# Gathering expert rows on one core: products moved from VectorE to GpSimd and ScalarE, rows fetched singly, and the paces of the side work redrawn

## The chip, the core and the metric

One NeuronCore of a Trainium2 chip runs the whole program. The metric is device time in microseconds from the first to the last instruction, a little more with what the launch adds. The engines are TensorE (PE, its weight loads as PEld), VectorE (DVE), ScalarE (ACT), GpSimd (POOL) and SyncE (SP, which issues most DMAs). Each engine takes its instructions strictly in the order that was written for it at build time; they wait for each other through semaphores.

## The reference, cut to what matters

Two blocks follow each other on 256 tokens of width 1024. The first has two layers of a three-part mixer and a feed-forward part (width 4096). The second has two layers of attention between the latent tokens `x` and 256 context tokens `xc`, each followed by a layer of 16,384 small experts, of which every token uses 128:

```python
def peer_block(hb, w_q, sub_keys, u_tab, v_tab):      # hb: tokens x 1024
    q = (hb @ w_q).reshape(n, 8, 256)
    s1, s2 = q[..., :128] . sub_keys[0], q[..., 128:] . sub_keys[1]
    ...                                               # top 16 of each, top 16 of the sums
    g = softmax(top_s)                                # 8 heads x 16 experts a token
    act = gelu(einsum('nhkd,nd->nhk', u_tab[expert], hb))
    return einsum('nhk,nhkd->nd', g * act, v_tab[expert])

for i in range(2):                                    # second block
    mod  = silu(c) @ ada_w[i] + ada_b[i]              # shifts, scales, gates for x
    modc = silu(c_ctx) @ ada_w[i] + ada_b[i]          # and for the context
    ...                                               # attention of x and, in layer 0, of xc
    x = x + g2 * peer_ffn(h2, ...)
    if i == 0:
        xc = xc + cg2 * peer_ffn(h2c, ...)
```

## The kernel before, in words

**Foreground.** `tile_two_blocks` writes the program in this order: mixer 0, feed-forward 0 ("ffn 0"), mixer 1, ffn 1, then `block2`: the attention of layer 0, its expert layer, and the same for layer 1. The experts are not looked up: all 128x128 of them are computed densely, one column of 128 at a time. `ahead` (line 1130) runs through 128 such columns e = 0 to 127: `hidden` loads 512 KB of the table u, splits it in two parts (ScalarE casts it, line 209, VectorE subtracts, line 210), multiplies it on TensorE with 384 tokens (24 matmuls of 384 columns, lines 243 to 245), applies GELU on ScalarE (line 1126) and stores the result. Beside it `choose` picks the experts, and `spread` (32 groups of 4 tokens for each 128 tokens) writes the gate table G: four comparisons a group on GpSimd (line 1071), four VectorE instructions (line 1075), eight small matmuls (line 1089) and a copy (line 1090). `experts` then weighs the stored columns with G and multiplies them with the table v.

**Side work.** Of the 256 context tokens, 128 join the 256 latent ones in these 384. The other 128 take the way of the reference: `gather` (line 1275), with one token on each partition. For each of the 128 choices a token has, one indirect DMA on GpSimd's queue (line 1286) fetches a row of u for every token, 128x1024 f32; VectorE multiplies it with the token's vector `h` and sums along the row into one number (line 1304). After GELU and gate, 128 rows of v are fetched in the same way, and VectorE adds each, times its number, to an accumulator (line 1308). Two rows share one place of 128x2x1024 and are fetched together, a pair ahead. `context`, `context_end`, `context_scores`, two `choose`, one `spread` and `gather` form one generator, `aside`; the foreground takes steps of it wherever it says `breathe`, or at the rates that the tables WM, WF, FN and GP give. `ada_rest` forms the modulation numbers: one 512 KB load and a VectorE product with sum (line 777) for each of 128 columns and vector.

**What sets the order.** A scheduler takes the instructions in the order in which the Python code wrote them as a priority, and fixes a sequence for each engine; an instruction whose inputs seem ready may be put ahead of older ones of the foreground. At run time nothing is reordered. The pool tags say how many places a tile has: `b8` 3 places of 8 KB a partition, `k8` 7, `wb` 3, `ws` 4 (two pairs of split weights).

Of the functions that the change touches:

Of the kernel before, what the change touches and what calls it, by code (L numbers as in the profile page):

```python
# [39 lines left out]
P0 = ((0, 1.0), (22, 1.0), (30, 0.8), (72, 0.8))  # L40
P1 = ((2, 1.0), (28, 0.8), (30, 0.72), (79, 0.8))

GP = (0.85, 0.6)
# [14 lines left out]
class Net:  # L58
    def __init__(self, ctx, tc, io):
        self.tc, self.nc, self.io = tc, tc.nc, io  # L60
        self.cst = ctx.enter_context(tc.tile_pool(name="cst", bufs=1))
        self.sb = ctx.enter_context(tc.tile_pool(name="sb", bufs=1))
        self.ps = ctx.enter_context(tc.tile_pool(name="ps", bufs=1, space=bass.MemoryType.PSUM))
        self.dr = ctx.enter_context(tc.tile_pool(name="dr", bufs=1, space=bass.MemoryType.DRAM))
        self.x = self.cst.tile([P, 2, D], F32, tag="x", name="x")
        for b in range(2):
            tc.nc.sync.dma_start(self.x[:, b], io["x"][b * P:(b + 1) * P])
        self.bufs = {"w": 4, "ws": 4, "wb": 3, "b8": 3, "b12": 2, "k8": 7, "k4": 4, "k2": 6, "b2": 3}
        self.pbufs = {"A": 2, "B": 2, "C": 4}
        self.uid = 0  # L70
        self.ring, self.turn = ("ws",), 0
        self.fg = Side("w", True, "C", "A", "k8", "k4", "k2", "f")
# [659 lines left out]
    def new_mod(self, l):  # L732
        self.mod = self.t("mod", [P, 2, 48], bufs=2)
        self.adab = self.load("adab", [P, 48], self.io["ada_b"][l], bufs=2)
        self.gn = self.load("gn", [P, 2, KC], self.io["norm2"][l], bufs=2)

    def ada_early(self):
# [17 lines left out]
        nc.vector.tensor_copy(self.mod[:, :, 0:EARLY], pt.rearrange("p f s -> p s f"))  # L755

    def ada_rest(self, i0, i1):

        nc, io = self.nc, self.io
        if i0 < 48 - 8:  # L760
            both = self.t("b12", [P, 2, D])
            cb = [both[:, i] for i in range(2)]
        else:
            cb = [self.t("kv", [P, D], bufs=2) for _ in range(2)]
# [3 lines left out]
        for i in range(i0, i1):  # L768
            l, f = divmod(i, 48)
            if f == 0:  # L770
                self.new_mod(1)
            w = self.load("wb", [P, D], io["ada_w"][i - EARLY])
            for s in range(2):
                if l and s and f >= 16:
                    continue
                junk = self.t("b2", [P, D], mybir.dt.bfloat16)
                nc.vector.scalar_tensor_tensor(junk, w, 1.0, cb[s], ALU.mult, ALU.mult, accum_out=self.mod[:, s, f:f + 1])
            if i == 47:
                nc.vector.tensor_add(self.mod[:, :, MID:], self.mod[:, :, MID:], self.adab[:, None, MID:].to_broadcast([P, 2, 48 - MID]))
            yield  # L780

    def modulation(self, l, part):

        nc, mod = self.nc, self.mod
        lo, hi, j, g = ((0, 16, 8, 0), (16, 48 if l else MID, 32, 1))[part]
        ns = 1 if l == 1 and part == 1 else 2
        for s in range(ns):
            nc.vector.tensor_add(mod[:, s, lo:hi], mod[:, s, lo:hi], self.adab[:, lo:hi])
            nc.vector.scalar_tensor_tensor(mod[:, s, j:j + 8], mod[:, s, j:j + 8], 1.0, self.gn[:, g], ALU.add, ALU.mult)
# [412 lines left out]
    def context(self):  # L1202
# [3 lines left out]
        mod = self.mod0 = self.mod  # L1206
# [5 lines left out]
        rest = self.ada_rest(EARLY, MID)  # L1212
# [62 lines left out]
    def gather(self, idx, g, out):  # L1275


        nc, io = self.nc, self.io
        tables = io["u_rows"], io["v"][0].rearrange("a b d -> (a b) d")
        work = [(t, c) for t in tables for c in range(0, P, 2)]  # L1280

        def fetch(i):
            t, c = work[i]
            r = self.t("b8", [P, 2, D])
            for j in range(2):
                nc.gpsimd.indirect_dma_start(out=r[:, j], out_offset=None, in_=t,
                                             in_offset=bass.IndirectOffsetOnAxis(ap=idx[:, c + j:c + j + 1], axis=0))
            return r

        hr = self.t("b8", [P, 2, D])  # L1290
        nc.sync.dma_start(hr[:, 0], self.hrd)
        h, acc = hr[:, 0], hr[:, 1]
        act = self.t("act", [P, P], bufs=1)
        r = fetch(0)
        for i, (t, c) in enumerate(work):
            if i == P // 2:
                nc.scalar.activation(act, act, AF.Gelu_apprx_tanh)
                nc.vector.tensor_mul(act, act, g)
            nxt = fetch(i + 1) if i + 1 < len(work) else None
            for j in range(2):  # L1300
                a = act[:, c + j:c + j + 1]
                if i < P // 2:
                    junk = self.t("b2", [P, D], mybir.dt.bfloat16)
                    nc.vector.scalar_tensor_tensor(junk, r[:, j], 1.0, h, ALU.mult, ALU.mult, accum_out=a)
                elif i == P // 2 and j == 0:
                    nc.vector.tensor_scalar(acc, r[:, j], a, None, ALU.mult)
                else:
                    nc.vector.scalar_tensor_tensor(acc, r[:, j], a, acc, ALU.mult, ALU.add)  # L1308
                yield
            r = nxt  # L1310
        nc.sync.dma_start(out, acc)
        yield

    def aside(self):


# [8 lines left out]
        yield from self.gather(idx, g, self.accd)  # L1325

    def block2(self, x):
# [7 lines left out]
        self.beside(self.attn_out(fg, 0, oT, col(mod, 0, 2), x), FN[3])  # L1335
        hx = self.norm_T(fg, x, col(mod, 0, 4), col(mod, 0, 3), lambda k: (h[0][:, k, 0:S], h[1][:, k, 0:S]))
        hd = lambda k: (h[0][:, k], h[1][:, k])
        far = self.side
        plan = self.routing(0, [hx], Gd[0], ((0, 0), (1, 8)), EAR[0], P0)
        self.ahead(0, hd, ND, self.kept, 128, plan + [(0, far, GP[0], False), (100, self.ada_rest(MID, 48), 0.3, True)])  # L1340
# [3 lines left out]
        rest, due = self.ada_rest(48, 96), [0.0]  # L1344

        def side(e):
            if e % 2:
                next(rest, None)
# [12 lines left out]
        mod = self.mod  # L1361
# [119 lines left out]
def tile_two_blocks(ctx: ExitStack, tc: tile.TileContext, io: dict, out: bass.AP):  # L1481
    net = Net(ctx, tc, io)
    x, net.out = net.x, out
    net.kept = net.dr.tile([128, P, ND], F32, tag="kept0", name="kept0")
# [24 lines left out]
```

## Time and profile before

| | us |
|---|---|
| median of 3 runs | 3633.68 |
| lowest, highest | 3614.31, 3634.95 |
| the profiled execution | 3624.63 |
| its span, first to last instruction | 3622.9 |

| engine | busy us | share of the span |
|---|---|---|
| PE | 3248.7 | 90% |
| PEld (beside PE) | 2772.2 | 77% |
| DVE | 2513.4 | 69% |
| ACT | 1449.4 | 40% |
| POOL | 978.2 | 27% |

Shares of the whole span hide the stages. In the trace, mixer 0 and ffn 0 take the first 556 us, mixer 1 lasts to 764, ffn 1 to 1032, attention and key scores of layer 0 to 1332, the 128 columns of `ahead` to about 2066, the expert sums to 2642, and layer 1 the rest. The fetches of `gather` lie between 1023 and 1882 us.

### The profile page before, as it was taken

To read this page: it belongs to the slowest core of one execution; us is meant where nothing else is said; L and a number is where in the kernel's file an instruction comes from. 1 tells how busy PE (TensorE), PEld (TensorE's weight loads), DVE (VectorE), ACT (ScalarE), POOL (GpSimd) and SP (SyncE) were. 2 spreads that over 40 slices of the span, in tenths; PEclk is the share of its full clock that TensorE was granted. 3 is DMA by queue.
4 is the path that set the end of the run, shared out by engine and by line. 5 is a ranking of instruction groups with operands and counts; after the bars stand their busy time and mean duration, and the time that the engine had idled before them with its cause. 6 is when DMAs were issued, how large, how long until landed. Compare 5 with 4: busy or idle time off the path is not lost. (4 is left out here: it accounts for less than half of the span.)

```text
span 3622.9 us, 51227 instructions
## 1 busy us (share of the span) xinstructions
PE 3248.7 (90%) x18333; PEld 2772.2 (77%) x18333; DVE 2513.4 (69%) x5177; ACT 1449.4 (40%) x2465; POOL 978.2 (27%) x968
## 2 busy tenths in 40 slices
PE   8999899889756698887779899999989999999999
PEld 6676688768644597887779887777868999988777
DVE  6667556789667897887665576655577888656665
ACT  6543245633323342232223433333344555454443
POOL 0000000000954434787776000000010067830000
PEclk9999999979978899998889999999999999999999
DMA  7456454325467778887886788877523677688885
GB/s 241 151 180 204 151 164 146 108 89 172 159 223 245 253 267 300 291 290 266 287 274 228 254 283 276 266 251 251 178 66 101 198 243 264 241 281 291 288 258 188
DMA packets 340225, 803.17 MB, mean 222 GB/s; under 512 B 31105, under 2 KB 179585, under 8 KB 334593
## 3 DMA queue, kind: packets, MB, share of 16 engines
q1 hardware_dynamic: 303104, 665.66, 56.0%
q0 software_dynamic: 36864, 134.23, 10.8%
q8 instruction: 144, 2.36, 0.3%
q14 instruction: 113, 0.92, 0.1%
HBM read 713.00 MB, written 86.77 MB: 221 GB/s over the span
## 5 line engine op out<-in xcount | busy, mean ns | idle before, releaser
L209 ACT CAST ws<-w 128x1024 fp32r<-128x1024 f32 (+1 forms) x528 | 547.3, 1037 | 1048.8 <-PE psA L244 727.6
L210 DVE TENSOR_TENSOR ws<-w,ws 128x1024 fp32r<-128x1024 f32 (+1 forms) x528 | 640.7, 1215 | 255.3 <-ACT ws L209 253.5
L245 PE MATMUL psA<-b,ws 128*128 128x384 f32 (+1 forms) x2048 | 659.0, 322 | 105.2 <-DVE ws L210 104.3
L1071 POOL TENSOR_SCALAR wb<-iota,R 128x128 f16<-128x128 f16 x640 | 600.3, 954 | 382.3 <-ACT R L1054 279.1
L243 PE MATMUL psA<-b,ws 128*128 128x384 f32 (+1 forms) x2048 | 663.4, 324 | 3.6 <-ACT ws L209 3.6
L244 PE MATMUL psA<-b,ws 128*128 128x384 f32 (+1 forms) x2048 | 652.1, 318 | 0.0
L245 PEld LDWEIGHTS psA<-b,ws 128*128 128x128 f32 x2048 | 398.9, 195 | 119.9 <-DVE ws L210 118.7
L209 ACT CAST k<-wb 128x1024 fp32r<-128x1024 f32 x256 | 269.0, 1051 | 513.3 <-DMA wb<-in_v 513.2
L245 PE MATMUL psC<-k,k 128*128 128x512 f32 x1056 | 422.7, 400 | 25.9 <-DVE k L210 25.2
L243 PE MATMUL psC<-k,k 128*128 128x512 f32 x1056 | 418.6, 397 | 19.6 <-ACT k L209 19.6
L244 PE MATMUL psC<-k,k 128*128 128x512 f32 x1056 | 417.6, 396 | 3.6 <-DVE k L210 3.6
L243 PEld LDWEIGHTS psA<-b,ws 128*128 128x128 f32 x2048 | 399.8, 195 | 4.7 <-ACT ws L209 4.5
L244 PEld LDWEIGHTS psA<-b,ws 128*128 128x128 f32 x2048 | 398.4, 195 | 0.0
L210 DVE TENSOR_TENSOR k<-wb,k 128x1024 fp32r<-128x1024 f32 x256 | 312.4, 1220 | 81.9 <-ACT k L209 81.7
L158 POOL TENSOR_TENSOR rsrf<-rsvf,neghalf 128x1 f32<-128x1 f32 (+5 forms) x38 | 41.9, 1106 | 1206.6 <-DVE rsvf L157 1206.6
L244 PE MATMUL psC<-ws,k 128*128 128x512 f32 (+1 forms) x608 | 250.3, 412 | 25.5 <-DVE ws L210 25.4
L245 PEld LDWEIGHTS psC<-k,k 128*128 128x128 f32 x1056 | 199.2, 189 | 93.2 <-DVE k L210 49.4
L1165 DVE TENSOR_TENSOR k<-k,b 128x384 f32<-128x384 f32 (+1 forms) x256 | 123.7, 489 | 202.7 <-DMA k<-kept 197.8
L243 PE MATMUL psC<-ws,k 128*128 128x512 f32 (+1 forms) x608 | 246.9, 410 | 7.1 <-DVE k L197 4.5
L243 PEld LDWEIGHTS psC<-k,k 128*128 128x128 f32 x1056 | 199.5, 189 | 66.7 <-ACT k L209 23.8
L1308 DVE SCALAR_TENSOR_TENSOR b<-b,act,b 128x1024 f32<-128x1024 f32 x127 | 164.2, 1293 | 120.3 <-DMA b<-in_v,idx 119.7
L245 PE MATMUL psC<-ws,k 128*128 128x512 f32 (+1 forms) x608 | 246.1, 407 | 0.7 <-DVE k L716 0.6
(452 smaller groups left out, 6096.2 us busy)
## 6 DMA issues: line engine op xcount, KB each, us to landing
w<-in_u SPq DMA_DIRECT2D x256, 512.0 KB
wb<-in_v SPq DMA_DIRECT2D x256, 512.0 KB
w<-in_w_ff SPq DMA_DIRECT2D x128, 512.0 KB
wb<-in_ada_w SPq DMA_DIRECT2D x80, 512.0 KB
G<-k SPq DMA_DIRECT2D x32, 1024.0 KB
w<-in_wA SPq DMA_DIRECT2D x48, 512.0 KB
kept<-k SPq DMA_DIRECT2D x128, 192.0 KB
b<-G SPq DMA_DIRECT2D x16, 1536.0 KB
```

What stands on the lines that cost most here:

```text
L158: nc.gpsimd.tensor_tensor(r[:m, :cols], v[:m, :cols], self.neghalf[:m, :cols], op=ALU.pow)
L209: self.nc.scalar.copy(hi, src)
L210: self.nc.vector.tensor_sub(lo, src, hi.bitcast(F32))
L243: self.nc.tensor.matmul(out, ah, bh, start=first, stop=False)
L244: self.nc.tensor.matmul(out, ah, bl, start=False, stop=False)
L245: self.nc.tensor.matmul(out, al, bh, start=False, stop=last)
L1071: nc.gpsimd.tensor_scalar(first[:, j], self.iota16, r0[:, n + j:n + j + 1], None, ALU.is_equal)
L1165: nc.vector.tensor_mul(g3, g3, Gs[:, :, j])
L1308: nc.vector.scalar_tensor_tensor(acc, r[:, j], a, acc, ALU.mult, ALU.add)
```

## The change

- `gather` works on single rows. Four places of 128x1024 take turns, and the fetch for row i+2 is issued at row i.
- For a row of u, GpSimd multiplies it with `h` in place (`TENSOR_TENSOR`), and one step later ScalarE sums it (a copy with an accumulator). VectorE has no part in it.
- Of the rows of v, the even ones are added by VectorE as before; the odd ones are scaled by ScalarE and added by GpSimd into a second accumulator, and GpSimd adds the two at the end.
- The expert choice for the gathered tokens comes first, and the first 96 steps of `gather` run beside the second `choose` and the 32 loads of `ada_rest` for layer 1; they are all written ahead of the second norm of layer 0. The `spread` for the 128 context tokens moves from `aside` (ffn 1) into `ahead`, which now has three of them.
- WM, WF, FN, P0 and GP get other numbers; of the `ada_rest` of layer 1, 16 columns stay beside the expert sums (of 48).

```diff
-WM = ({3: 1, 5: 2, 12: 3, 22: 1, 34: 1}, {12: 2, 14: 2, 18: 2, 22: 2, 26: 2, 32: 2, 34: 2, 37: 2})
-WF = ((0, 2.0), (0, 3.5))
-FN = (4, 2.0, 2.0, 2.0)
+WM = ({3: 4, 4: 1, 5: 2, 9: 1, 11: 1, 12: 3, 14: 1, 16: 1, 18: 1, 20: 1, 22: 2, 24: 1, 26: 1, 30: 1, 32: 1, 34: 1},
...
+WF = ((0, 1.6), (0, 1.6))
+FN = (2, 1.8, 1.8, 1.8)
...
-    def gather(self, idx, g, out):
+    def gather(self, idx, g, hr):
...
+            def fetch(i):
+                if i < i1:
+                    nc.gpsimd.indirect_dma_start(out=places[i % 4], out_offset=None, in_=(u, v)[i // P],
+                                                 in_offset=bass.IndirectOffsetOnAxis(ap=idx[:, i % P:i % P + 1], axis=0))
+
+            def first(i):
+                r, c = places[i % 4], i % P
+                if i < P:
+                    nc.gpsimd.tensor_tensor(r, r, h, op=ALU.mult)
+                elif c % 2 == 0:
+                    nc.vector.scalar_tensor_tensor(acc[:, 0], r, act[:, c:c + 1], acc[:, 0], ALU.mult, ALU.add)
+                else:
+                    nc.scalar.activation(r, r, AF.Copy, scale=act[:, c:c + 1])
+
+            def second(i):
+                r, c = places[i % 4], i % P
+                if i < P:
                     junk = self.t("b2", [P, D], mybir.dt.bfloat16)
-                    nc.vector.scalar_tensor_tensor(junk, r[:, j], 1.0, h, ALU.mult, ALU.mult, accum_out=a)
...
+                    nc.scalar.activation(junk, r, AF.Copy, accum_out=act[:, c:c + 1])
+                elif c % 2:
+                    nc.gpsimd.tensor_tensor(acc[:, 1], acc[:, 1], r, op=ALU.add)
...
+            fetch(i0), fetch(i0 + 1)
+            for i in range(i0, i1):
+                if i > i0:
+                    second(i - 1)
+                fetch(i + 2)
...
+                first(i)
                 yield
...
         idx, g = yield from self.choose(self.rc, ss[1], True)
-        R = yield from self.choose(self.rc, ss[0])
-        yield from self.spread(R, self.Gd[0], 16, "B", "b8")
...
+        def weights():
+            self.R0 = yield from self.choose(rc8, ss[0])
+            yield from self.ada_rest(1, 16, 48, [hr[:, 1]])
...
+        for i, _ in enumerate(steps(0, NA, [two[i // 2][:, i % 2] for i in range(4)])):
+            next(also, None)
+            yield
...
-        self.ahead(0, hd, ND, self.kept, 128, plan + [(0, far, GP[0], False), (100, self.ada_rest(MID, 48), 0.3, True)])
+        plan += [(P0[4][0], self.spread(self.R0, Gd[0], 16), P0[4][1], True), (0, far, GP[0], False)]
+        self.ahead(0, hd, ND, self.kept, KEPT0, plan + [(96, self.ada_rest(0, MID, 48), 0.4, True)])
```

GpSimd's queue in ffn 1, before (`wb` holds a group's one-hot tiles, `iota` and `R` what they are compared from):

```order
L158 TENSOR_TENSOR rsrf_6646<-rsvf_6645,neghalf 128x1
L158 TENSOR_TENSOR rsrf_6652<-rsvf_6651,neghalf 128x1
L1071 TENSOR_SCALAR wb_8118<-iota_225,R_1535_8111 128x128 x4
L1071 TENSOR_SCALAR wb_8126<-iota_225,R_1535_8111 128x128 x4
L1071 TENSOR_SCALAR wb_8219<-iota_225,R_1535_8111 128x128 x4
L1071 TENSOR_SCALAR wb_8237<-iota_225,R_1535_8111 128x128 x4
```

The same stretch of GpSimd's queue now (`b_1381` and `k_1382` are the four row places, `b_1379` is `h`):

```order
L1293 DMA k_1382_7113<-in_u_rows,idx_7104 128x1024
L1299 TENSOR_TENSOR b_1381_7112<-b_1381_7112,b_1379_7109 128x1024
L1293 DMA k_1382_7113<-in_u_rows,idx_7104 128x1024
L1299 TENSOR_TENSOR b_1381_7112<-b_1381_7112,b_1379_7109 128x1024
L1293 DMA b_1381_7112<-in_u_rows,idx_7104 128x1024
L1299 TENSOR_TENSOR k_1382_7113<-k_1382_7113,b_1379_7109 128x1024
```

The 128 comparisons have gone from ffn 1 and the fetches and products of u, one of each in turn, stand in their place; before, the fetches of u began only behind the comparisons.

ScalarE's queue in ffn 1 now (line 216 is the cast that was line 209, line 1309 the row sum, line 721 a square of the foreground, line 714 before):

```order
L1309 ACTIVATE b_1569_8235,act_7111<-b_1381_7112 128x1024
L216 CAST ws_7497<-w_7495 128x1024
L1043 ACTIVATE k_1383_7118<-k_1383_7118 128x128
L1309 ACTIVATE b_1580_8317,act_7111<-b_1381_7112 128x1024
L216 CAST ws_7515<-w_7513 128x1024
L721 ACTIVATE k_1417_7319<-k_1439_7465 128x256
L721 ACTIVATE k_1417_7319<-k_1440_7470 128x256
L1309 ACTIVATE b_1581_8325,act_7111<-k_1382_7113 128x1024
L216 CAST ws_7543<-w_7541 128x1024
```

A row sum stands ahead of nearly every weight cast; before, casts and squares alone followed each other there. In the order now all 128 row sums stand ahead of the first column of `ahead`.

GpSimd's queue in the first half of `ahead` now (line 1311 is the add of an odd row of v, line 1076 the comparisons that were line 1071, `b_2032` and `b_2033` the row places):

```order
L1293 DMA b_2032_10222<-in_v,idx_7104 128x1024 x2
L1076 TENSOR_SCALAR wb_12147<-iota_225,R_1676_8902 128x128 x4
L1311 TENSOR_TENSOR b_1379_7109<-b_1379_7109,b_2033_10223 128x1024
L1293 DMA b_2033_10223<-in_v,idx_7104 128x1024 x2
L1076 TENSOR_SCALAR wb_12204<-iota_225,R_1676_8902 128x128 x4
L1311 TENSOR_TENSOR b_1379_7109<-b_1379_7109,b_2032_10222 128x1024
L1293 DMA b_2032_10222<-in_v,idx_7104 128x1024 x2
```

Before, this part of the queue held fetches of u and then of v, later with comparisons between them, and no product or sum; the comparisons of the third `spread` are new here.

## Rows read from the trace of the kernel before

**Rows 1.** Stretches: from:to, length, each engine's busy us, TensorE's granted clock, DMA share, GB/s
```profile
764.00:1032.00 268.00, 224.57 (x1427) 188.03 (x1425) 216.22 (x588) 102.37 (x148) 112.45 (x132) 0.94 0.50 163
1032.00:1332.00 300.00, 211.19 (x1032) 171.78 (x1033) 249.69 (x563) 99.99 (x216) 130.39 (x110) 0.82 0.74 251
1332.00:1641.00 309.00, 268.29 (x1501) 258.59 (x1500) 255.07 (x578) 96.82 (x143) 197.60 (x173) 0.93 0.84 287
1641.00:2071.00 430.00, 357.01 (x2088) 342.16 (x2086) 252.65 (x323) 136.77 (x204) 258.91 (x238) 0.92 0.78 263
2642.00:2816.00 174.00, 160.95 (x889) 135.75 (x889) 126.78 (x364) 87.76 (x219) 9.48 (x12) 0.96 0.29 93
```
**Rows 2.** TensorE's waits, 1332 to 1641, 1641 to 2071: us in total, times, longest
```profile
PE psA L245 <- DVE ws L210: 38.7, 16, 5.4
...
PE psA L245 <- DVE ws L210: 65.0, 22, 7.2
```
**Rows 3.** VectorE's groups in those two stretches: busy us, mean ns, idle us before
```profile
L1308 DVE SCALAR_TENSOR_TENSOR b<-b,act,b 128x1024 f32<-128x1024 f32 x56 | 72.3, 1291 | 33.9 <-DMA b<-in_v,idx 33.7
L1304 DVE SCALAR_TENSOR_TENSOR b<-b,b 128x1024 bf16<-128x1024 f32 x30 | 36.3, 1216 | 15.0 <-DMA b<-in_u_rows,idx 14.9
...
L1308 DVE SCALAR_TENSOR_TENSOR b<-b,act,b 128x1024 f32<-128x1024 f32 x71 | 92.0, 1295 | 86.4 <-DMA b<-in_v,idx 86.0
```
**Rows 4.** ScalarE's GELU, one a column: 1332 to 1640.6, 1640.6 to 2071
```profile
L1126 ACT ACTIVATE k<-psA 128x384 f32<-128x384 f32 x56 | 27.1, 485 | 0.0
...
L1126 ACT ACTIVATE k<-psA 128x384 f32<-128x384 f32 x72 | 35.0, 486 | 0.0
```
**Rows 5.** ScalarE, 1917.9 to 1992.5, then 2036.5 to 2061.9: columns, and groups of spread
```profile
L1126 ACT ACTIVATE k<-psA 128x384 f32<-128x384 f32 x16 | 7.8, 487 | 0.0
L1090 ACT ACTIVATE k<-psC 128x512 f32<-128x512 f32 x13 | 7.7, 592 | 0.0
...
L1126 ACT ACTIVATE k<-psA 128x384 f32<-128x384 f32 x6 | 2.9, 486 | 0.0
```
**Rows 6.** GpSimd's groups of the whole span, then the comparisons of ffn 1 alone
```profile
L1286 POOL DMA_INDIRECT b<-in_v,idx x128 | 165.3, 1291 | 106.4 <-DVE b L1308 51.4 <-issue 26.0 <-DVE k L946 16.0
L1286 POOL DMA_INDIRECT b<-in_u_rows,idx x128 | 157.4, 1230 | 222.3 <-DVE b L1304 137.6 <-DVE amxf L892 22.5 <-issue 20.1
...
L1071 POOL TENSOR_SCALAR wb<-iota,R 128x128 f16<-128x128 f16 x128 | 108.9, 869 | 133.8 <-ACT R L1054 133.5 <-POOL wb L1071 0.2
```
**Rows 7.** Lines 1071 and 210 alone: ns shortest/median/longest, first and last start
```profile
L1071 POOL TENSOR_SCALAR wb<-iota,R x640: 592/702/4086, 913.4 to 3209.8; 128x128 f16<-128x128 f16 x160
...
L210 DVE TENSOR_TENSOR ws<-w,ws x128: 1200/1219/1436, 1331.2 to 2062.2; 128x1024 fp32r<-128x1024 f32 x128
```
**Rows 8.** VectorE's 128-column cast (1500 to 1900 us) and its 128x1024 subtract (ffn 1)
```profile
L1016 DVE CAST k<-k 128x128 f32<-128x128 uint32 x4 | 1.0, 248 | 0.0
...
L210 DVE TENSOR_TENSOR ws<-w,ws 128x1024 fp32r<-128x1024 f32 x64 | 78.2, 1222 | 18.6 <-ACT ws L209 18.2
```
**Rows 9.** Line 713, the first VectorE instruction on each product of ffn 1
```profile
L713 DVE TENSOR_SCALAR k<-psA x32: 395/418/425, 796.1 to 1033.8; 128x256 f32<-128x256 f32 x32
```
**Rows 10.** VectorE in 1032 to 1332: the gathered rows' products, and the reads of their sums
```profile
L1304 DVE SCALAR_TENSOR_TENSOR b<-b,b 128x1024 bf16<-128x1024 f32 x97 | 117.8, 1222 | 38.5 <-DMA b<-in_u_rows,idx 38.5
L1304 DVE DVE_READ_ACCUMULATOR b<-b,b 128x1 f32 x97 | 8.2, 84 | 0.0
```
**Rows 11.** ScalarE: a 128x1024 cast in ffn 1, an accumulator's read in 1032 to 1332
```profile
L209 ACT CAST ws<-w 128x1024 fp32r<-128x1024 f32 x65 | 68.1, 1048 | 112.2 <-PE psC L244 50.1 <-PE psA L244 42.5 <-DVE ws L210 5.6
...
L839 ACT ACTIVATION_READ_ACCUMULATOR k<-psC 128x1 f32 x20 | 4.4, 221 | 0.0
```
**Rows 12.** TensorE's waits in the expert sums, 2071 to 2642
```profile
PE psC L245 <- DVE k L210: 18.2, 23, 2.0
PE psC L243 <- ACT k L209: 9.1, 3, 6.9
```
**Rows 13.** The page: GB/s in 40 slices of the span; the software queue (256 fetches): packets, MB
```profile
GB/s 241 151 180 204 151 164 146 108 89 172 159 223 245 253 267 300 291 290 266 287 274 228 254 283 276 266 251 251 178 66 101 198 243 264 241 281 291 288 258 188
...
q0 software_dynamic: 36864, 134.23, 10.8%
```

More of the change, by code (lines that the diff above doesn't have):

```diff
@@ L754, in ada_early, with ada_rest @@
             nc.tensor.transpose(pt[:, f], row[:, f * P:(f + 1) * P], self.ident[0:2, 0:2])
-        nc.vector.tensor_copy(self.mod[:, :, 0:EARLY], pt.rearrange("p f s -> p s f"))
-    def ada_rest(self, i0, i1):
+        nc.vector.tensor_copy(self.mods[0][0][:, :, 0:EARLY], pt.rearrange("p f s -> p s f"))
+    def ada_rest(self, l, f0, f1, cb=None):
         nc, io = self.nc, self.io
[L760 to L764, printed above, removed]
+        if cb is None:
+            if l == 0 and f0 < MID:
+                both = self.t("b12", [P, 2, D])
+                cb = [both[:, i] for i in range(2)]
+            else:
+                cb = [self.t("kv", [P, D], bufs=2) for _ in range(2)]
         for t, n in zip(cb, ("c", "c_ctx")):
@@ L767, in ada_rest @@
             nc.scalar.activation(t, t, AF.Silu)
[L768 to L775, printed above, removed]
+        if l not in self.mods:
+            self.new_mod(l)
+        mod, adab, _ = self.mods[l]
+        for f in range(f0, f1):
+            w = self.load("wb", [P, D], io["ada_w"][48 * l + f - EARLY])
+            for s, c in enumerate(cb):
                 junk = self.t("b2", [P, D], mybir.dt.bfloat16)
-                nc.vector.scalar_tensor_tensor(junk, w, 1.0, cb[s], ALU.mult, ALU.mult, accum_out=self.mod[:, s, f:f + 1])
-            if i == 47:
-                nc.vector.tensor_add(self.mod[:, :, MID:], self.mod[:, :, MID:], self.adab[:, None, MID:].to_broadcast([P, 2, 48 - MID]))
+                nc.vector.scalar_tensor_tensor(junk, w, 1.0, c, ALU.mult, ALU.mult, accum_out=mod[:, s, f:f + 1])
+            if l == 0 and f == 47:
+                nc.vector.tensor_add(mod[:, :, MID:], mod[:, :, MID:], adab[:, None, MID:].to_broadcast([P, 2, 48 - MID]))
             yield
     def modulation(self, l, part):
-        nc, mod = self.nc, self.mod
+        nc, (mod, adab, gn) = self.nc, self.mods[l]
         lo, hi, j, g = ((0, 16, 8, 0), (16, 48 if l else MID, 32, 1))[part]
@@ L1211, in context @@
         yield
-        rest = self.ada_rest(EARLY, MID)
+        rest = self.ada_rest(0, EARLY, MID)
         def both():
@@ L1309, in gather @@
                 yield
-            r = nxt
-        nc.sync.dma_start(out, acc)
-        yield
+            second(i1 - 1)
+        return steps
     def aside(self):
+        nc = self.nc
         yield from self.context()
@@ L1321, in aside @@
         idx, g = yield from self.choose(self.rc, ss[1], True)
-        R = yield from self.choose(self.rc, ss[0])
-        yield from self.spread(R, self.Gd[0], 16, "B", "b8")
+        hr = self.t("b8", [P, 2, D])
+        nc.sync.dma_start(hr[:, 0], self.hrd)
+        steps = self.gather(idx, g, hr)
+        rc8 = Side("wb", True, "B", "B", "k8", "wb", "b2", "b", "wb", "b2")
+        def weights():
+            self.R0 = yield from self.choose(rc8, ss[0])
+            yield from self.ada_rest(1, 16, 48, [hr[:, 1]])
+        also = weights()
+        two = [self.t(t, [P, 2, D]) for t in ("b8", "k8")]
+        for i, _ in enumerate(steps(0, NA, [two[i // 2][:, i % 2] for i in range(4)])):
+            next(also, None)
+            yield
+        self.done(also)
+        self.early = True
+        yield
+        two = [self.t("b8", [P, 2, D]) for _ in range(2)]
+        yield from steps(NA, 2 * P, [two[i // 2][:, i % 2] for i in range(4)])
         self.accd = self.dr.tile([P, D], F32, tag="accd", name="accd")
-        yield from self.gather(idx, g, self.accd)
+        nc.gpsimd.tensor_tensor(hr[:, 0], hr[:, 0], hr[:, 1], op=ALU.add)
+        nc.sync.dma_start(self.accd, hr[:, 0])
+        yield
     def block2(self, x):
@@ L1335, in block2 @@
         self.beside(self.attn_out(fg, 0, oT, col(mod, 0, 2), x), FN[3])
+        far = self.side
+        while not self.early:
+            next(far)
         hx = self.norm_T(fg, x, col(mod, 0, 4), col(mod, 0, 3), lambda k: (h[0][:, k, 0:S], h[1][:, k, 0:S]))
         hd = lambda k: (h[0][:, k], h[1][:, k])
-        far = self.side
         plan = self.routing(0, [hx], Gd[0], ((0, 0), (1, 8)), EAR[0], P0)
-        self.ahead(0, hd, ND, self.kept, 128, plan + [(0, far, GP[0], False), (100, self.ada_rest(MID, 48), 0.3, True)])
+        plan += [(P0[4][0], self.spread(self.R0, Gd[0], 16), P0[4][1], True), (0, far, GP[0], False)]
+        self.ahead(0, hd, ND, self.kept, KEPT0, plan + [(96, self.ada_rest(0, MID, 48), 0.4, True)])
         gates = self.t("k8", [P, 4, 512])
```

62 lines of the change are left out of this document (25 added, 37 removed).

## The prediction, made before the changed kernel ran

> **What bounds the kernel now.** I read the table of stretches first [rows 1]. Its five engine columns are TensorE, its weight loads, VectorE, ScalarE and GpSimd; then come the granted clock, the share of the DMA engines' time and GB/s. VectorE leads in the attention of layer 0 (1032 to 1332 us), TensorE elsewhere, but TensorE is not full in the first half of `ahead`, from 1332 to 1641 us (268 of 309), and in the second half (357 of 430). GpSimd is not full anywhere: 112 of 268 us in ffn 1, 198 of 309 and 259 of 430 in `ahead`. So I asked what TensorE waits for in `ahead` [rows 2]: the weight split that VectorE does, 38.7 and 65.0 us. Why VectorE is late stands in its own groups [rows 3]: in the queue ahead of the splits are the multiply-adds of gathered rows, and before those VectorE sat idle for fetches: 33.9 + 15.0 us in the first half, 86.4 in the second. A late row thus holds the split, and the split holds TensorE. That is what the change can win.
>
> What can it win at most? The GELU, one a column, counts columns [rows 4]: 56 up to 1640.6, 72 after it. After the gather is over, 6 columns without a group of `spread` took 25.4 us, or 4.23 each, and 16 columns with 13 groups 74.6 us [rows 5], so a group adds (74.6 − 16×4.23)/13 = 0.53. All 128 columns with the 64 groups of now would take 575 us at that pace, and they took 730.
>
> **The change part by part.** What GpSimd must do before which column I read off the built order, by following what each instruction needs back through the queues. Between the first square of ffn 1 (796.1 us, from [rows 9], where line 713 starts at once on the first finished product) and the first GELU of `ahead` (1332.2), GpSimd now has 120 fetches of u, 8 of v, 124 products and 16 comparisons. From there to the GELU of column 56 it has 116 fetches of v, 58 adds and 212 comparisons. Behind that are 156 comparisons in 39 groups and no gather.
>
> Prices: a fetch of u 1.23, of v 1.29, and a comparison 0.869 as in ffn 1 [rows 6]. A GpSimd product or sum of 128x1024 f32 stands nowhere in the trace, so I bound it. Low end: VectorE's own 1.22 for such a product [rows 10]. High end: eight comparisons of 128 columns at 0.592, the shortest of them, as if none of it were a fixed cost: 4.74 [rows 7]. A middle by ratio, the root of 1.22×4.74, is 2.40; another one, GpSimd's 592 ns against VectorE's 248 ns on 128 columns [rows 8], times 1.22, is 2.92. I take 2.40 for the product by itself, and add the wait that the comparisons of ffn 1 had beside VectorE, 0.869 − 0.592 = 0.28: **2.68**.
>
> Term 1, from 796.1 to 1332.2: 120×1.23 + 8×1.29 + 16×0.869 = 172 of GpSimd, and 124×2.68 = 332 more: 504 for the 536 of before, **−32**. That it is GpSimd which ends this stretch follows from what is left of the others. VectorE had 224.6 + 249.7 in the two stretches, of which 126.0 go (97 products and the reads of their sums, [rows 10]); the part behind 796.1 is some 224.6×236/268 + 123.7 = 322. The DMAs of ffn 1 become 64 weights, some 75 fetches and 27 loads of the modulation, 0.524 MB each, 87 MB; at the best slice of the page, 300 GB/s [rows 13], 290 us. (The software queue's 134.23 MB over 256 fetches are the 0.524.) The attention of layer 0 without a gather may come down towards that of layer 1, 174 us [rows 1]. None of the three reaches 504.
>
> Term 2, from the first column to column 56: 116×1.29 + 212×0.869 = 334, and 58×2.68 = 155: 489 for 308.6, **+180**. Here the change puts more on GpSimd than the first half of `ahead` had time for: comparisons of a third `spread`, and adds of odd rows. TensorE, which needs 56×4.23 = 237 plus its groups, waits.
>
> Term 3, from column 56 to the end of `ahead`: no gather is left to hold the split; 71×4.23 + 39×0.53 = 321 for the 421 of before, **−100**. The cover here is gone only if rows of v are still fetched behind column 58.
>
> Term 4, the expert sums: 16 columns of the modulation instead of 48, so 32 loads and up to as many VectorE products less. TensorE waited 18.2 + 9.1 us there for the split [rows 12]; I take half, **−14**.
>
> At nothing, with the cover named: the 128 row sums and 64 scalings of ScalarE, 128×(1.048 + 0.221) + 64×1.05 = 230 us [rows 11]. ScalarE is busy for 102 + 100 us of the 568 from 764 to 1332, so it has the room; what it hasn't is freedom of order. A place comes free when its sum is done, and the fetch that wants it is one step (3.9 us) behind the product; if the sum stands behind a cast that waits for TensorE, GpSimd waits too. Its casts waited 112 us for others in ffn 1 [rows 11], so I hold this for up to +40 and put it in the range. The longer lead of the fetches also goes at nothing: from issue to use are three fetches and two products, 9.1 us. Mixer 0, ffn 0, mixer 1 and layer 1 get some steps earlier or later, TensorE's work is the same: 0, give or take 20. TensorE's granted clock was 0.82 in 1032 to 1332, where it was busy least, and 0.92 to 0.96 in the others [rows 1]; if the thinner first half of `ahead` falls to that, it costs nothing there, since GpSimd ends that stretch.
>
> Sum: 3624.6 − 32 + 180 − 100 − 14 = **3659 us**, made against the profiled execution; against the median of the runs, 3633.7, it is 0.7% more. In general it is 3172 + 182 × the price of a GpSimd product, so the price decides: under 2.34 is faster by 1%, over 2.74 slower by 1%. About 1% is what a measurement of this kernel can tell from no change.
>
> The Trainium skill, in "GPSIMD Engine Reference", section "Elementwise — side-by-side cycle accounting", gives 4497 ns for a GpSimd add of 2048 f32 values a partition, 1.96 times VectorE's. An estimate from that page for 1024 is 2.25 us, and with the same 0.28 of wait the sum would be 3632.
>
> **The rivals.**
>
> *A cheap product.* If GpSimd is little dearer than VectorE, the products hide. For it: a fetch and a product of 1.22 alternate at 2.45 us. Then term 1 falls to what ffn 1's DMAs and the attention need, 290 + 174 − 32 = 432, −104; term 2 is 334 + 58×1.22 = 405, +96: 3624.6 − 104 + 96 − 100 − 14 = **3503**. At 2.0 it is 3172 + 364 = 3536. Against it: the same engine takes 592 ns for 128 columns where VectorE takes 248 [rows 7, 8].
>
> *A dear product.* At 2.92 the sum is 3703; at 4.74 it is 4034. For it: a comparison, with an eighth of the columns, takes half as long as VectorE's whole product, and up to 4.09 [rows 7].
>
> *VectorE held off.* While GpSimd works on 1024 columns, a VectorE instruction that reads two operands from SBUF may be unable to start. Then the weight split (line 210), which TensorE waits for already [rows 2], is what gets late, and VectorE becomes the bound of term 1: its 322 us plus 2.40 for each product that holds it off. It decides from (504 − 322)/2.40 = 76 of the 124 products on; with all 124 it takes 620 in place of 504: **3775**, slower by 3.9%. Against it: beside comparisons the split took 1.22 in the middle, 1.436 at most [rows 7], so it lost 0.2 there. For it: comparisons themselves were stretched from 0.59 to 0.87, so the two engines do meet.
>
> The Trainium skill has a rule for this, in "SBUF — State Buffer", section "Who interferes with whom": a VectorE instruction with two inputs from SBUF contends with a GpSimd instruction that reads SBUF, and whichever is first keeps the shared pair of ports to its end, while the other stands still. By that rule the split would lose up to a whole product; the trace shows GpSimd's side of it (0.59 to 0.87), and on VectorE's side 0.2 us at most.
>
> *The change does not do what it says.* If the scheduler's order let `gather` slip behind, v would still be fetched in the second half and term 3 would not come; the built order speaks against it, and I give it no chance of its own.
>
> **How the numbers follow.** The forecast, price 2.5 to 2.9 and 3627 to 3700: 0.42. Cheap, below 2.34 and 3500 to 3597: 0.28. Dear, above 2.9: 0.17. VectorE held off: 0.13. Faster by over 1% is the cheap case, 0.28. Within 1%, up to 3670 or a price of 2.74, is 0.28 of the forecast's 0.42; slower is its other 0.14 with the last two, 0.44. Both signs hold much, so the forecast's own range stands here: 3627 to 3700. The 8-in-10 range runs from 3530 (a price of about 2.0), leaving 0.07 of the cheap case below, to 3785, which takes in VectorE held off and a price of 3.35, leaving 0.12 above.
>
> **What would show it.** Duration of GpSimd's `TENSOR_TENSOR` of 128x1024: near 2.7, all else follows from it. GpSimd busy for over 95% from 796 to column 56, and TensorE's waits there ending at GpSimd, directly or through `spread`'s copies. GELUs 8.7 us apart up to column 56 and 4.5 after. If instead VectorE's line 216 (the split) grows beyond 1.44 beside products, the third rival is right. If GpSimd sits idle before fetches for row sums, ScalarE's order sets the pace, which I priced at nothing. If the columns after 56 stay at 5.8, term 3 is wrong.

## The result, and the profile after

The changed kernel takes 3822.12 us, the median of 4 runs (3815.36 to 3830.2), against 3630.22 for the kernel before in 4 runs: 1.054 times its time (95% interval 1.050 to 1.058), slower by 5.4%. Its profiled execution has a span of 3822.0. The forecast was 3659, with 3785 as the upper end of its range.

The table of stretches of the changed kernel answers to [rows 1], with the same columns (length; busy us of TensorE, its weight loads, VectorE, ScalarE, GpSimd; granted clock, DMA share, GB/s). Its rows are ffn 1, the attention and key scores, `ahead` up to column 56, `ahead` after it, and the expert sums:

```profile
761.00:1104.00 343.00, 233.95 (x1177) 198.79 (x1175) 309.56 (x462) 153.67 (x245) 256.10 (x133) 0.84 0.71 238
1104.00:1433.70 329.70, 210.19 (x1053) 175.05 (x1053) 244.07 (x404) 170.23 (x348) 274.25 (x162) 0.81 0.58 192
1433.70:1938.30 504.60, 329.14 (x1767) 301.37 (x1768) 335.39 (x615) 174.37 (x236) 471.82 (x386) 0.82 0.67 226
1938.30:2283.00 344.70, 330.12 (x2055) 321.84 (x2053) 164.58 (x237) 137.41 (x203) 168.75 (x163) 0.97 0.66 218
2283.00:2849.00 566.00, 545.31 (x2313) 439.33 (x2314) 323.56 (x475) 192.69 (x271) 1.12 (x2) 0.98 0.70 220
```

ffn 1 has grown from 268 to 343 us, and VectorE is busy for 310 of them where it was for 216, though it has no more work of its own there than before (310 less the 121 found below is 189). That is the surprise. From the first product of ffn 1 (794.0) to the first column of `ahead` (1433.7) it is now 640 us where 536 were, and 504 were forecast. The first half of `ahead` went nearly as forecast: 505 us for 489, GpSimd busy for 472 of them. Its GELUs, ScalarE's rows that answer to [rows 4], stand for 56 columns from 1433.7 and 72 from 1938.3 (mean ns, then idle before):

```profile
L1131 ACT ACTIVATE k<-psA 128x384 f32<-128x384 f32 x56 | 26.9, 480 | 0.0
...
L1131 ACT ACTIVATE k<-psA 128x384 f32<-128x384 f32 x72 | 35.1, 488 | 1.5 <-PE psA L252 1.5
```

That is 9.0 us a column, then 4.8. GpSimd's own groups of the whole span give the price that was missing; they answer to [rows 6]:

```profile
L1299 POOL TENSOR_TENSOR b<-b,b 128x1024 f32<-128x1024 f32 x80 | 201.3, 2520 | 41.9 <-DMA b<-in_u_rows,idx 41.0
...
L1311 POOL TENSOR_TENSOR b<-b,b 128x1024 f32<-128x1024 f32 x64 | 154.6, 2416 | 6.1 <-ACT b L1303 5.1
L1299 POOL TENSOR_TENSOR k<-k,b 128x1024 f32<-128x1024 f32 x48 | 117.7, 2456 | 29.0 <-DMA k<-in_u_rows,idx 28.4
```

A GpSimd product takes 2.42 to 2.52 us, less than the 2.68 of the forecast. By the forecast's own formula (3172 + 182 × price) some 3620 would have come out. So the price is not what went wrong. VectorE's groups of ffn 1 show what did; [rows 8, 9] have their like of before:

```profile
L217 DVE TENSOR_TENSOR ws<-w,ws 128x1024 fp32r<-128x1024 f32 x65 | 122.1, 1883 | 23.7 <-ACT ws L216 23.6
L782 DVE SCALAR_TENSOR_TENSOR b<-wb,b 128x1024 bf16<-128x1024 f32 x24 | 43.8, 1836 | 4.1 <-DMA wb<-in_ada_w 4.1
L723 DVE TENSOR_TENSOR k<-k,k 128x256 fp32r<-128x256 f32 x30 | 31.9, 1099 | 0.0
L722 DVE TENSOR_TENSOR k<-k 128x256 f32<-128x256 f32 x30 | 23.9, 834 | 2.9 <-ACT k L721 2.9
L720 DVE TENSOR_SCALAR k<-psA 128x256 f32<-128x256 f32 x30 | 11.3, 411 | 1.4 <-PE psA L252 1.3
```

The weight split (line 217; the prediction calls it line 216) takes 1.88 us in the mean where it took 1.22. Lines 722 and 723, two inputs from SBUF, take 2 and 2.6 times the 0.42 that they take in a run without products (run 1 below), while line 720, which reads PSUM, takes 0.41 as ever. One piece of the time line of both engines shows what happens (start, length, instruction):

```profile
972.51 1.78 POOL L1293 DMA_INDIRECT b<-in_u_rows,idx  x1 [0.16 <-issue]
973.37 0.74 DVE L720 TENSOR_SCALAR k<-psA 128x256 f32<-128x256 f32 x2
974.03 8.36 DVE L217 TENSOR_TENSOR ws<-w,ws 128x1024 fp32r<-128x1024 f32 x1
974.31 7.00 POOL L1299 TENSOR_TENSOR b<-b,b 128x1024 f32<-128x1024 f32 x3
...
982.32 0.74 DVE L722 TENSOR_TENSOR k<-k 128x256 f32<-128x256 f32 x2
```

Three products follow each other on GpSimd from 974.31 to 981.31, and one split of VectorE lies over all three: 8.36 us instead of 1.22. It ends 1.08 us behind the last of them. So do the others: each of the 38 splits between 761 and 1434 us that took over 1.5 us ends 1.08 to 1.10 us behind the end of a product. I summed, over VectorE's instructions that overlap a product, their length less that of the undisturbed ones of the same form: 121 us between 761 and 1104 and 87 up to 1434, in 95 instructions that lost over 0.3 us each. These 208 us are the theory to test.

### The profile page after: what moved, and what is told of

It reads as the page before. It is cut to its first block, busy times and chain, and to the rows that moved or that the text cites. A ratio compares the mean times of both kernels' runs of the same rounds, so it can differ in the third digit from the quotient of the medians.

```text
span 3822.0 us, 51290 instructions
## 1 busy us (share of the span) xinstructions
PE 3286.5 (86%) x18333; PEld 2808.3 (73%) x18333; DVE 2575.0 (67%) x4857; ACT 1649.8 (43%) x2785; POOL 1458.5 (38%) x1162
## 5 line engine op out<-in xcount | busy, mean ns | idle before, releaser
L217 DVE TENSOR_TENSOR ws<-w,ws 128x1024 fp32r<-128x1024 f32 (+1 forms) x528 | 733.4, 1390 | 332.0 <-ACT ws L216 329.5
L252 PEld LDWEIGHTS psA<-b,ws 128*128 128x128 f32 x2048 | 405.8, 198 | 138.6 <-DVE ws L217 138.2
L250 PEld LDWEIGHTS psA<-b,ws 128*128 128x128 f32 x2048 | 406.1, 198 | 74.3 <-ACT k L1131 43.8
L251 PEld LDWEIGHTS psA<-b,ws 128*128 128x128 f32 x2048 | 405.9, 198 | 0.0
L252 PEld LDWEIGHTS psC<-k,k 128*128 128x128 f32 x1056 | 200.7, 190 | 78.3 <-DVE k L217 32.8
L250 PEld LDWEIGHTS psC<-k,k 128*128 128x128 f32 x1056 | 200.6, 190 | 59.4 <-ACT k L216 14.6
L251 PEld LDWEIGHTS psC<-k,k 128*128 128x128 f32 x1056 | 200.9, 190 | 46.0
```

The lines of the kernel that those rows point to most:

```text
L217: self.nc.vector.tensor_sub(lo, src, hi.bitcast(F32))
L250: self.nc.tensor.matmul(out, ah, bh, start=first, stop=False)
L251: self.nc.tensor.matmul(out, ah, bl, start=False, stop=False)
L252: self.nc.tensor.matmul(out, al, bh, start=False, stop=last)
```

## The experiments

**H** says that VectorE's instructions are held off by GpSimd's products, and that this makes the stretch up to the first column long. **Q** says that GpSimd's own queue, and the row sums that ScalarE must do in its order, set it. For the first half of `ahead`, **G** says that GpSimd's load sets it, **L** that the landing of fetched rows does. All times below are us; "first" is the start of the first column's GELU, "to 56" the time from there to column 56's, and "56 to 127" the time from that to column 127's.

| kernel | median | ratio to before (95%) | first | to 56 | 56 to 127 |
|---|---|---|---|---|---|
| before | 3630 | 1 | 1332 | 309 | 421 |
| changed | 3822 | 1.054 (1.050 to 1.058) | 1434 | 505 | 339 |
| 1 u: writes for products | 3698 | 1.018 (1.015 to 1.021) | 1270 | 478 | 401 |
| 2 u on VectorE | 3662 | 1.009 (1.006 to 1.012) | 1249 | 479 | 381 |
| 3 v on VectorE | 3697 | 1.018 (1.014 to 1.022) | 1434 | 333 | 382 |
| 4 third spread late | 3792 | 1.045 (1.042 to 1.047) | 1422 | 433 | 385 |
| 5 u and v on VectorE | 3531 | 0.973 (0.969 to 0.977) | 1253 | 338 | 399 |
| 6 the same, third spread late | 3557 | 0.981 (0.979 to 0.983) | 1251 | 297 | 456 |
| 7 products in halves | 3843 | 1.059 (1.057 to 1.061) | 1468 | 498 | 334 |
| 8 v: writes for adds | 3776 | 1.042 (1.040 to 1.044) | 1426 | 417 | 374 |
| 9 as 5, spare products | 3774 | 1.038 (1.036 to 1.040) | 1460 | 366 | 402 |
| 10 as 5, spare writes | 3613 | 0.995 (0.993 to 0.997) | 1300 | 345 | 409 |
| 11 as 5, lead of three | 3541 | 0.974 (0.972 to 0.976) | 1253 | 333 | 403 |
| 12 as 11, third spread eased | 3545 | 0.976 (0.974 to 0.977) | 1250 | 318 | 422 |

**1. Products that read nothing.**

```diff
-                    nc.gpsimd.tensor_tensor(r, r, h, op=ALU.mult)
+                    nc.gpsimd.memset(r, 0.0)
+                    nc.gpsimd.memset(r, 0.0)
+                    nc.gpsimd.memset(r[:, :512], 0.0)
```

> Each GpSimd product of a row of u is replaced by three GpSimd memsets of the same place (1024, 1024 and 512 columns, some 2.3 us in all by the 1.83 us that one of 2048 columns took): GpSimd is busy as long and the places change hands as before, but nothing is read from SBUF. The products are left out, so the sums are of zeros. Theory H (VectorE held off by products): the weight splits of ffn 1, 1.88 us in the mean now, fall back to 1.2 to 1.3, and the 208 us that VectorE's instructions lost between 761 and 1434 us are gone; the rows of u, 5.2 us apart now, come at GpSimd's own pace of 3.8 to 4.2, and the first column of `ahead` starts at 1280 to 1330 in place of 1434; total 3600 to 3720. Theory Q (GpSimd's own queue and the sums that ScalarE must do in its order set the pace, and VectorE's losses lie beside that): GpSimd's load is the same, the rows stay some 5 us apart, the first column starts behind 1400; the order drawn for this kernel puts 32 fetches of v behind column 56, worth at most 80 us, so the total is 3740 to 3820.

Measured 3698, in H's range; the first column starts at 1270, a little under its 1280 to 1330. VectorE in 761 to 1104 us, the rows that answer to those of the changed kernel above:

```profile
L217 DVE TENSOR_TENSOR ws<-w,ws 128x1024 fp32r<-128x1024 f32 x81 | 98.9, 1226 | 40.1 <-ACT ws L216 39.6
...
L722 DVE TENSOR_TENSOR k<-k 128x256 f32<-128x256 f32 x32 | 12.2, 419 | 1.6 <-ACT k L721 1.6
L723 DVE TENSOR_TENSOR k<-k,k 128x256 fp32r<-128x256 f32 x32 | 12.2, 419 | 0.1
...
L907 DVE TENSOR_SCALAR k<-k,asmf 128x512 f32<-128x512 f32 x9 | 10.9, 1229 | 0.0
L1021 DVE CAST k<-k 128x128 f32<-128x128 uint32 x4 | 7.2, 1794 | 0.0
```

GpSimd's three memsets, whole span, for 80 of the 128 rows:

```profile
L1300 POOL MEMSET b<- 128x1024 f32 x80 | 77.1, 965 | 0.1
...
L1299 POOL MEMSET b<- 128x1024 f32 x80 | 76.7, 964 | 23.8 <-DMA b<-in_u_rows,idx 23.8
...
L1301 POOL MEMSET b<- 128x512 f32 x80 | 43.2, 541 | 0.1
```

964 + 965 + 541 is 2.47 us for a row, as long as a product, and ScalarE's sums are all there. Yet the splits are back at 1.23, VectorE loses about 40 us by the same count in place of 208, and the first column starts 164 us earlier. Not all of it is H's: this kernel's order puts 12 rows of u behind the first column, and at the 4.47 us a row that it takes these are worth up to 54. Some 110 remain. The rows come 4.47 apart, not 3.8 to 4.2, so a smaller part lies elsewhere. One piece may be the steps' own pace: run 2, with no product on GpSimd there, still has 4.04. Another is Q's: the foreground's norms need a small instruction of GpSimd's (line 165), and it stands in the queue behind rows of u. VectorE waited for it here, up to the first column (us in total, times, longest):

```profile
DVE k L182 <- POOL rsrf L165: 45.7, 2, 42.4
```

In the changed kernel these waits are 32 us (lines 182 and 863), in run 5 they are 1. Q as the whole cause, with 3740 or more, falls.

**2. u back on VectorE.**

```diff
-                    nc.gpsimd.tensor_tensor(r, r, h, op=ALU.mult)
+                    junk = self.t("b2", [P, D], mybir.dt.bfloat16)
+                    nc.vector.scalar_tensor_tensor(junk, r, 1.0, h, ALU.mult, ALU.mult, accum_out=act[:, c:c + 1])
```

(ScalarE's sums are dropped with it.)

> Products and sums of the rows of u go back to VectorE (one instruction with a sum), the rest is as changed: single rows, lead of two steps, the paces, odd rows of v on ScalarE and GpSimd. Theory H: no product holds VectorE off; VectorE has 322 us and 120 x 1.31 between the first product of ffn 1 and the first column, 480, so that stretch takes 480 to 560 in place of 640, and the total is 3650 to 3740. Theory Q: GpSimd loses 120 x 2.4 and ScalarE all sums, so the stretch falls as well, to the 536 of before or less: 3640 to 3720. The two differ little here; the run shows what moving u off VectorE costs as a whole.

Measured 3662, in both ranges. The stretch to the first column takes 456 us, under H's 480 to 560. The first column starts at 1249, 83 us before that of the kernel before: early rows, single places and the new paces together are worth this, once nothing holds VectorE off; no run tells them apart. Moving u off VectorE costs 160 us.

**3. v back on VectorE.**

```diff
-                elif c % 2 == 0:
+                else:
                     nc.vector.scalar_tensor_tensor(acc[:, 0], r, act[:, c:c + 1], acc[:, 0], ALU.mult, ALU.add)
-                else:
-                    nc.scalar.activation(r, r, AF.Copy, scale=act[:, c:c + 1])
...
-                elif c % 2:
-                    nc.gpsimd.tensor_tensor(acc[:, 1], acc[:, 1], r, op=ALU.add)
```

> All rows of v are added by VectorE, none is scaled by ScalarE or added by GpSimd; u stays as changed. Theory G (GpSimd's load, 472 of 505 us, sets the first 56 columns): 58 adds of 2.4 us leave GpSimd there, and the order has 76 fetches of v ahead of column 56 in place of 124; 505 falls to 300 to 360, columns 56 to 127 rise from 339 to some 370, total 3640 to 3720. Rival L (the landing of the fetched rows sets it: ScalarE waited 321 us for rows of v in the 57 waits, and the wait only moves to VectorE): the columns stay 8 to 9 us apart, total 3780 to 3830.

Measured 3697: G. In the changed kernel the longest entries of ScalarE's and of TensorE's waits in the first half of `ahead` were these (us in total, times, longest):

```profile
ACT b L1303 <- DMA b<-in_v,idx: 321.2, 57, 11.3
...
PE psA L252 <- DVE ws L217: 107.1, 42, 6.9
```

ScalarE stood 321 us before its scalings, waiting for rows whose fetch was late because GpSimd issued it late. Without the adds the stretch falls from 505 to 333, where GpSimd is busy for 307 (the order also leaves 70 fetches of v in it, for 113):

```profile
1433.50:1766.20 332.70, 288.29 (x1786) 274.63 (x1785) 278.57 (x633) 113.62 (x178) 307.17 (x280) 0.91 0.80 274
1766.20:2148.20 382.00, 333.93 (x2034) 321.93 (x2032) 220.28 (x283) 129.81 (x193) 230.70 (x211) 0.94 0.76 258
```

The wait named "DMA" was thus for the most part a wait for the engine that issues the DMA.

**4. The third spread later.**

```diff
-P0 = ((0, 1.0), (22, 1.0), (32, 1.0), (66, 0.8), (0, 1.0))
+P0 = ((0, 1.0), (22, 1.0), (32, 1.0), (66, 0.8), (57, 1.0))
```

> One number: the third spread starts at column 57, not at column 0, so 128 comparisons leave the first 56 columns for the later ones, where GpSimd was busy for 169 of 345 us. Theory G: 128 x 0.87 = 111 us less up to column 56, 505 falls to some 395; behind it 32 groups more at 0.53 each, +17; total 3715 to 3745. Rival L (landing of fetched rows): the pace up to column 56 stays, total 3800 to 3840.

Measured 3792, between both. GpSimd's load up to column 56 fell by 100 us, the stretch by 72; behind it 46 were given back, not 17. GpSimd was no longer full (371 of 433), and it waited 22 us for rows that ScalarE had yet to scale. With the comparisons out of the way the landing begins to show: G, with some L behind it.

**5. u and v on VectorE**: the edits of 2 and 3.

> All products and sums of u and of v on VectorE, the rest as changed: single rows in four places, lead of two, early rows of u, third spread in `ahead`, the paces. If the two parts add (u back: first column at 1249 in place of 1434; v back: 333 us for the first 56 columns in place of 505, 382 for 43 us more behind them), the total is 3822 - 160 - 127 = some 3535, at 3500 to 3570, and faster than before by 2 to 3%. If one bound lies behind both (VectorE too full in ffn 1 and in `ahead` once it does all of it), the first 56 columns take over 400 and the total is 3600 to 3660.

Measured 3531: the two parts add, and this version beats both kernels, by 2.7% and 7.6%. Its stretches, 761 to the first column, to column 56, and to column 127:

```profile
761.00:1252.90 491.90, 404.42 (x2232) 339.57 (x2230) 465.91 (x1085) 187.27 (x334) 180.15 (x140) 0.91 0.80 276
1252.90:1590.70 337.80, 286.20 (x1784) 269.92 (x1784) 276.50 (x649) 113.98 (x177) 315.16 (x288) 0.92 0.81 269
1590.70:1990.10 399.40, 344.21 (x2034) 330.25 (x2032) 239.75 (x299) 129.91 (x194) 255.85 (x224) 0.93 0.80 267
```

With all the products of u back, VectorE is busy for 466 us up to the first column; without them, in the changed kernel, it was busy for 554. The work that was taken off it cost it more than it had weighed.

**6. The same with the third spread late** (the edit of 4).

> As the one with all on VectorE, and the third spread starts at column 57 besides. GpSimd's 128 comparisons leave the first 56 columns, which then take 270 to 310; behind them 32 groups more beside some 54 rows of v, 390 to 430. Theory: the two stretches trade, total within 20 us of the kernel with all on VectorE. Rival: the first stretch is bound by the fetches and not by comparisons, so it stays near 330 and the total is 30 to 60 us higher than that kernel's.

Measured 3557, 26 more than 5, between the 20 of the theory and the 30 of its rival. The first 56 columns take 297, as the theory said, so GpSimd's comparisons did bind there; the others take 456, above its 430.

**7. Products in halves.**

```diff
-                    nc.gpsimd.tensor_tensor(r, r, h, op=ALU.mult)
+                    for q in range(2):
+                        nc.gpsimd.tensor_tensor(r[:, 512 * q:512 * q + 512], r[:, 512 * q:512 * q + 512], h[:, 512 * q:512 * q + 512], op=ALU.mult)
```

> Each GpSimd product of a row of u in two instructions of 512 columns; the same data read and written. Theory H (a product holds a VectorE instruction with two inputs until it ends): each hold is half as long, so of the 208 us lost by VectorE between 761 and the first column 80 to 120 are gone, unless VectorE is passed over by the second half as well; the rows of u come 4.5 to 4.8 us apart in place of 5.0, total 3760 to 3800. Theory Q (GpSimd's own queue and the sums set the pace): 128 instructions more at some 0.1 each, the same or slower, 3820 to 3850.

Measured 3843, slower. The half products take 1.38 in the mean:

```profile
L1300 POOL TENSOR_TENSOR b<-b,b 128x512 f32<-128x512 f32 x160 | 217.1, 1381 | 34.6 <-DMA b<-in_u_rows,idx 33.6
```

By the same count as above VectorE loses 215 us up to the first column, no less than the 208. Where a split waits and a second product follows the first at once, the split is mostly not let in between: it was passed over at 31 of 38 such places, in the changed kernel at 6 of 7. That was the clause in H's expectation ("passed over by the second half as well"), and the three products in a row above are the same thing. This run by itself would have spoken for Q.

**8. Adds of v that read nothing** (the three memsets in place of the add).

> The 64 GpSimd adds of odd rows of v are each replaced by three memsets of the row's place, 2.4 us in all (the odd rows are left out of the sum); u stays as changed. The order has 99 fetches of v ahead of column 56, not 124, and 44 adds' worth, not 60: by GpSimd's load alone (theory G) the first 56 columns take 505 x 401/472 = 430, at 420 to 445. If VectorE's instructions held off by the adds (75 us between 1434 and 1938) count as well (theory H), 370 to 410. In both the splits there come back from 1.51 to 1.23. Total 3780 to 3810 by G, 3750 to 3780 by H.

Measured 3776, in H's range; 417 up to column 56, between the two ranges, with GpSimd busy for 384, less than the 401 that G's range was made from. The splits are back at 1.23. By the load as it came G gives 505 × 384/472 = 411, so the 88 us gained need nothing of H. G holds there; that VectorE's losses add a little in that half isn't ruled out.

**9 and 10. Contention added to the fast version.** To kernel 5, behind each row of u, a spare instruction on the spent row; first a product, then three memsets:

```diff
+                if i < P:
+                    nc.gpsimd.tensor_tensor(r, r, h, op=ALU.mult)
```

> The kernel with all products on VectorE, and behind each row of u a spare GpSimd product of that row with h, 2.4 us, whose result nobody uses; the counts of fetches and products ahead of each column are those of that kernel. GpSimd has room for them: 181 + 114 x 2.4 = 455 of the 492 us from 761 to the first column. Theory H: the spare products hold VectorE's two-input instructions off; the splits of ffn 1 go from 1.22 to 1.6 to 2.2 in the mean, VectorE (541 busy of 492 plus what it loses) gets later by 80 to 200 us, total 3610 to 3740. Theory Q: what is spare and fits into GpSimd's idle time costs what the wait for each row costs, 0 to 50, as in the run with spare writes beside it; total 3530 to 3580.

> The same with three memsets of the spent row (2.4 us in all) in place of the spare product: GpSimd as busy, nothing read. Theory H: no instruction of VectorE's is held off, splits 1.22, total within 0 to 50 of the kernel with all on VectorE (3531): 3530 to 3580, and 70 to 180 below the run with spare products. Theory Q: the same as that run, within 20 us.

Measured 3774 and 3613: 243 and 82 us over kernel 5, each above its range, and 161 apart, inside the 70 to 180 of H. Spare writes cost more than thought, since each waits for VectorE's instruction on the row and the next fetch stands behind it. What reads adds 161 to that, so Q, which had the two within 20 us, falls again. VectorE's splits in 761 to 1104 us, with spare products:

```profile
L217 DVE TENSOR_TENSOR ws<-w,ws 128x1024 fp32r<-128x1024 f32 x73 | 128.0, 1755 | 13.5 <-ACT ws L216 13.4
```

and with spare writes:

```profile
L217 DVE TENSOR_TENSOR ws<-w,ws 128x1024 fp32r<-128x1024 f32 x79 | 96.5, 1221 | 11.2 <-ACT ws L216 10.6 <-issue 0.2
```

**11 and 12. A longer lead, and an eased third spread,** on kernel 5:

```diff
-            fetch(i0), fetch(i0 + 1)
+            fetch(i0), fetch(i0 + 1), fetch(i0 + 2)
...
-                fetch(i + 2)
+                fetch(i + 3)
```

(12 also starts the third spread at column 16, at 0.5 a column.)

> The kernel with all on VectorE, rows fetched with a lead of three steps in the same four places. There VectorE waited 8 + 51 + 73 us in `ahead` for rows under way. If the lead is what they lack, half or more of the 132 goes and TensorE's waits for the split (105 us) fall likewise: total 3470 to 3515. If the fetches wait for their turn on GpSimd or for the memory instead (the queue's order sets it), within 15 us of 3531.

> As with the lead of three, and the third spread starts at column 16 with a group every other column, so that GpSimd's 315 of 338 us up to column 56 become some 270 and the groups lie evenly. The first 56 columns 290 to 310, the others 390 to 420: total 10 to 30 us below the run with the lead of three alone; if the earlier trade repeats (third spread wholly behind column 56: +26), 0 to 15 us above it.

Measured 3541 and 3545, their intervals overlapping that of kernel 5; 12 did not get the 10 to 30 us below 11. VectorE still waits 8 + 45 + 71 us for rows in 11, some 124 for the 132 of 5: the lead is not what they lack. What sets those waits stays open.

## Why the prediction was wrong

The terms, each against the profiled executions:

| | forecast | measured |
|---|---|---|
| mixers, ffn 0 | 0 | −2 |
| 1: ffn 1's first product to the first column | −32 | +104 (640 for 536) |
| 2: to column 56 | +180 | +196 (505 for 309) |
| 3: to column 127 | −100 | −82 (339 for 421) |
| 4: to layer 1's first column | −14 | −12 |
| layer 1 | 0 | −4 |
| sum | +34 | +199 |

**The step that failed is term 1**: "None of the three reaches 504." VectorE's 322 us there were its old load less the products of u, each remaining instruction at its old length. They did not keep that length. The stretch, columns as in [rows 1]:

```profile
794.00:1433.70 639.70, 420.71 (x2113) 354.37 (x2113) 527.98 (x773) 306.11 (x560) 515.74 (x285) 0.82 0.65 217
```

VectorE was busy for 528 us. Less the 208 by which products held its instructions off, some 320 are left, as forecast. GpSimd, which was to end the stretch at 95% and more, was busy for 516 of 640; it waited for row sums and, 63 us, for rows under way.

**The rival that named it was right in mechanism, and its sum came near partly by luck.** VectorE held off by products gave 620 for term 1 and 3775 in all; 640 and 3822 came, and its sign came too, the split beyond 1.44 (1.88). But its 620 took a whole product of 2.40 for each of 124, 298 us, where the trace has 208. What makes up the rest is VectorE idle for 112 us, 51 of them before splits whose cast ScalarE had yet to do and 32 for GpSimd's part of the norms. It had 0.13, because beside the comparisons the split had lost 0.2 us at most [rows 7]. That row was read too far. A comparison is 0.59 us long and a product 2.4; a hold lasts as long as the instruction that holds, and longer where several stand in a row. And the comparisons' own stretching, 0.59 to 0.87, showed that the two engines meet. The trace of before says it more sharply: in ffn 1 the 32 comparisons that met no VectorE instruction with two inputs from SBUF took 0.60 us, and the 90 that met one for over 0.1 us took 0.98 in the mean.

The Trainium skill's rule on this ("SBUF — State Buffer", section "Who interferes with whom": two SBUF inputs on VectorE against a GpSimd instruction that reads, the first one keeps the ports) agrees with the trace in which instructions are held: of what overlaps a product, splits and lines 722 and 723 stretch, while line 720 from PSUM takes 0.41 and does not. Which came first can't be read off the starts: 11 of the 38 held splits have a start up to 0.6 us ahead of the product's. Not in that rule, but in the trace, is that a waiting split is mostly passed over again by a product that follows at once.

**Terms 2 and 3 were right in mechanism.** GpSimd's load set the first half (runs 3, 4 and 8, in 4 with some waiting for rows): 505 for the 489 of the forecast. Behind it 4.8 us a column in place of 4.5. **The price** of a product was bounded by 1.22 and 4.74 and taken as 2.68; 2.42 to 2.52 came, 2.33 at the shortest. That 2.40, a middle between bounds so far apart, lay near it was luck; the 0.28 of wait was too much. The cover named for ScalarE's sums held only in part: GpSimd waited 36 us for sums in all, within the 40 that the range held for it.

## What to carry to other kernels

Work moved from VectorE to GpSimd is not off VectorE if it reads SBUF: 128 products of 1.22 us taken away cost VectorE 208 us of standing still. Before such a move, list what VectorE still has with two inputs in SBUF at that time, and charge it the length of the GpSimd instructions that it will meet, not the little that short ones cost it before. What the foreground itself needs of GpSimd waits in the same queue. And where a wait names a DMA, ask first whether the engine that issues it is full.

## What the hardware showed that I had not expected

- A VectorE instruction that waits for GpSimd is mostly not served between two GpSimd instructions that follow at once (passed over at 6 of 7 such places, with halved products at 31 of 38): 8.36 us for a split of 1.22, over three products. Halving the products changed nothing in the loss (215 for 208 us).
- GpSimd loses little by it: its product takes 2.42 to 2.52 in the mean, 2.33 at the shortest.
- GpSimd's writes do not hold two-input instructions (splits 1.23 beside memsets), but they hold some with one SBUF input: in run 1 the cast of 128 columns took 1.79 in the mean where it took 0.25 [rows 8], and line 907, 512 columns, 1.23 where it took 0.49 before.
- TensorE's granted clock was 0.81 to 0.84 in all the stretches where it waited most (busy for 64 to 68% of them), and 0.97 right behind them; each is a mean over stretches at its two levels, full speed and half.
